# mLSTM heads of a hybrid layer: token sums by a two-column stationary operand, factors turned by DRAM, and carried keys weighted and summed on VectorE

## The chip, the core and the metric

The kernel runs on one core of one Trainium2 chip. The metric is device time in microseconds (us) of one execution, the median of several runs; lower is better. Engines are named as in the profile: PE (TensorE matmuls), PEld (its weight loads), DVE (VectorE), ACT (ScalarE), POOL (GpSimd), SP (SyncE, which issues every DMA here).

## The reference, cut to what matters

The layer runs four mLSTM heads and eight forgetting-attention heads side by side on 1024 tokens of width 1024, then a projection, cross-attention into 256 memory tokens, a squared-ReLU MLP and a final norm. The change is in the mLSTM heads (128 wide each), which the reference computes so:

```python
def body(carry, xs):
    C, n, m = carry
    ...
    scores = jnp.einsum('bhtd,bhsd->bhts', qc, kc) * jnp.exp(dmat - m_t[..., None])
    inter = jnp.exp(m_inter - m_t)
    num = (jnp.einsum('bhts,bhsd->bhtd', scores, vc)
           + inter[..., None] * jnp.einsum('bhed,bhtd->bhte', C, qc))
    den = scores.sum(-1) + inter * jnp.einsum('bhd,bhtd->bht', n, qc)
    h = num / jnp.maximum(jnp.abs(den), jnp.exp(-m_t))[..., None]
    ...
    C_new = decay[..., None, None] * C + jnp.einsum('bhs,bhse,bhsd->bhed', wa, vc, kc)
    n_new = decay[..., None] * n + jnp.einsum('bhs,bhsd->bhd', wa, kc)
...
mh = mh * lax.rsqrt(jnp.mean(mh * mh, axis=-1, keepdims=True) + EPS)
mh = mh * ml_norm[l].astype(jnp.float32).reshape(ML_HEADS, ML_DH)
ml_out = (mh.reshape(B, S, ML_W) * jax.nn.sigmoid(ml_o.astype(jnp.float32))).astype(x.dtype)
```

For each token two sums are needed: `den`, a sum over the weighted scores, and the mean square of the head's 128 outputs. Together they give one factor per token and head.

## The kernel before

Activations lie with the model's width on the partitions and tokens along the free axis. A matmul of fp32 accuracy is three passes over operands that are split into a high and a low part (`mm3`, lines 184 to 188); the split itself is an ACT copy that rounds (L134 or L137) and a DVE subtraction (L135 or L138). A projection tile of 128 outputs by 512 tokens is 24 matmuls of 512 columns into one PSUM bank. Banks are handed out by `mm()` in the rotation mm, tp, m2, tp: a bank is free again when DVE has taken the last result out of it.

An mLSTM head is worked in two halves of 512 tokens, each a chunk of its own. For each head `ml_project` runs the key projection, its convolution and SiLU (`conv_silu`, L505 to L513), a forgetting-attention projection, `carried` (the state after the first half), the query projection with its convolution, another forgetting-attention projection, `carry` (state times queries of the second half: L557, L562, L563) and the output gate. Then `ml_head` (a generator) does the scores and sums of both halves; its closing part, which scales the outputs by the factors and stores them, is stepped between the pieces of the next head's `ml_project` (`closing`, `next(closing)`), and for the last head between pieces of the attention's value projection.

Inside `ml_head`, per half: scores into PSUM (`sp`), weights by ACT (L587, from the row broadcast `nmb` in tile r_a, loaded by L576), a mask by POOL (L589), the product by DVE (L590), the split, the running sum `acc` by POOL (L594) and the weighted values into `num` (bank ov). After the last key block come `nsb` (L600), its square `sq` (L601), and `sum_cols` (L217) on `acc` and on `sq`: for each 128 tokens a matmul with those 128 columns as stationary operand and the constant column `ones` moving, so that a sum lands as one column with 128 tokens on the partitions. Eight columns of `dens` and of `sqs` hold the 1024 tokens of a head. The factor `fac` comes out of these (L612 to L618) as 128 by 8; `to_row` (L249 to L253) turns it with a PE transpose, an ACT copy, a store to DRAM (`facd`) and a broadcast load into r_a, and L626 loads the second half's broadcast. L629, L630, L137 and L138 make the scaled output and its split, L633 and L634 store it to `mix`.

`carried` (L519 to L552) transposes the keys y on PE (L527), multiplies them by weights per token on DVE while it takes them out of PSUM (L529), splits them, multiplies them with the values (L540), and sums them per key dimension with four more matmuls against `ones` (L542).

Tile buffers are few: r_a and r_y have one each, r_c, r_d, r_e and r_p two each, the PSUM score bank `sc` three. The framework orders each engine's instructions ahead of time; what stands in a row waits for what stands above it on that engine, DMA issues on SP too. SP keeps a strict order: an issue whose data are not ready holds those behind it.

## Time and profile before

| | us |
|---|---|
| median of 3 runs | 1521.66 (1521.24 to 1523.61) |
| the profiled execution: its time | 1523.35 |
| the profiled execution: its span in the trace | 1521.6 |
| DVE busy | 1100.3 (72%) |
| ACT busy | 727.7 (48%) |
| POOL busy | 510.1 (34%) |

The span runs from the first to the last instruction of the trace; what lies around it is 1.75 us of this execution's time. The mLSTM heads fill roughly 80 to 390 us of the span; the score phase of the forgetting attention runs beside the last head's end from about 355 us on. The lines that carry the argument stand in the prediction.

### The profile page before, as it was taken

What the parts mean: (1) busy time and instruction counts of PE and PEld (TensorE: products, weight loads), DVE (VectorE), ACT (ScalarE), POOL (GpSimd) and SP (SyncE); (2) the same over time, 40 slices, a digit from 0 to 9 for tenths busy, and PEclk for the clock granted to TensorE, in tenths of its full rate; (3) what the DMA queues carried; (4) which work ended last, traced back from release to release, by engine and by line L of the source; (5) the groups of instructions that cost most, each with busy time, mean ns of one, the idle gap of its engine ahead of it and who ended that gap; (6) DMA issues with size and microseconds to landing.
All of it is one profiled execution on the core that took longest, in us unless ns stands there. A gap on an engine that the chain in (4) does not pass through costs nothing.

```text
span 1521.6 us, 21977 instructions
## 1 busy us (share of the span) xinstructions
PE 1502.7 (99%) x7694; PEld 1261.5 (83%) x7694; DVE 1100.3 (72%) x1743; ACT 727.7 (48%) x1360; POOL 510.1 (34%) x543
## 2 busy tenths in 40 slices
PE   9999999999999999999999999999999999999997
PEld 9988888889999788888888877778787888888887
DVE  7766676765787786944457989898887667787665
ACT  7324343334687665644443456666664621122124
POOL 1003030413364442511110034544555265663322
PEclk9999999999999999999999999999999999999999
DMA  6322223435888886843344437776678777776623
GB/s 239 109 77 87 98 100 114 135 126 157 246 244 267 260 264 230 300 131 124 119 147 157 153 134 277 247 256 242 222 252 286 291 277 276 276 270 248 239 94 111
DMA packets 122538, 299.86 MB, mean 197 GB/s; under 512 B 13614, under 2 KB 28264, under 8 KB 115516
## 3 DMA queue, kind: packets, MB, share of 16 engines
q1 hardware_dynamic: 122428, 298.46, 57.4%
q8 instruction: 60, 0.98, 0.3%
q14 instruction: 50, 0.41, 0.1%
HBM read 199.60 MB, written 98.81 MB: 196 GB/s over the span
## 4 chain that ended last, share of the span: by engine, by line
PE 93%; DVE 3%; ACT 2%; DMA 1%; issue 1%; SPq 0%; DVEq 0%; POOLq 0%; POOL 0%; ACTq 0%
PE tp L186 8%; PE tp L187 8%; PE tp L188 8%; PE m L186 6%; PE sc L186 6%; PE m L187 6%; PE m L188 6%; PE sc L187 6%; PE sc L188 6%; PE mm L186 6%; PE mm L187 6%; PE mm L188 6%; PE ov L186 2%; PE ov L187 2%; PE ov L188 2%; PE ov L801 2%
## 5 line engine op out<-in xcount | busy, mean ns | idle before, releaser
L186 PE MATMUL tp<-act,wl 128*128 128x512 f32 (+1 forms) x440 | 172.9, 393 | 1.2 <-ACT row L1396 0.7
L187 PE MATMUL tp<-act,wh 128*128 128x512 f32 (+1 forms) x440 | 172.1, 391 | 0.0
L188 PE MATMUL tp<-act,wh 128*128 128x512 f32 (+1 forms) x440 | 171.7, 391 | 0.0
L135 DVE TENSOR_TENSOR wl<-wr,wh 128x1024 fp32r<-128x1024 f32 (+2 forms) x95 | 124.5, 1311 | 22.0 <-ACT wh L134 21.4
L134 ACT ACTIVATE wh<-wr 128x1024 fp32r<-128x1024 f32 (+2 forms) x95 | 95.6, 1007 | 75.9 <-PE tp L188 34.7
L186 PE MATMUL mm<-act,wl 128*128 128x512 f32 (+1 forms) x332 | 127.5, 384 | 0.0
L188 PE MATMUL mm<-act,wh 128*128 128x512 f32 (+1 forms) x332 | 127.3, 383 | 0.0
L187 PE MATMUL mm<-act,wh 128*128 128x512 f32 (+1 forms) x332 | 127.2, 383 | 0.0
L186 PE MATMUL m<-act,wl 128*128 128x512 f32 (+1 forms) x308 | 117.7, 382 | 0.5 <-DVE wl L135 0.5
L188 PE MATMUL m<-act,wh 128*128 128x512 f32 (+1 forms) x308 | 117.7, 382 | 0.0
L187 PE MATMUL m<-act,wh 128*128 128x512 f32 (+1 forms) x308 | 117.5, 381 | 0.0
L186 PEld LDWEIGHTS tp<-act,wl 128*128 128x128 f32 x440 | 82.6, 188 | 20.6 <-ACT row L1396 1.2
L188 PEld LDWEIGHTS tp<-act,wh 128*128 128x128 f32 x440 | 82.6, 188 | 18.9
L187 PEld LDWEIGHTS tp<-act,wh 128*128 128x128 f32 x440 | 82.7, 188 | 18.5
L186 PE MATMUL sc<-act,wl 128*128 128x512 f32 (+1 forms) x248 | 97.0, 391 | 1.0 <-DVE wl L135 1.0
L188 PE MATMUL sc<-act,wh 128*128 128x512 f32 (+1 forms) x248 | 96.7, 390 | 0.0
L187 PE MATMUL sc<-act,wh 128*128 128x512 f32 (+1 forms) x248 | 96.6, 390 | 0.0
L1467 POOL TENSOR_TENSOR z<-wr 128x256 f32<-128x256 f32 x56 | 51.7, 944 | 130.6 <-DMA wr<-w_ff2q 116.8
L134 ACT ACTIVATE wh<-z 128x1024 fp32r<-128x1024 f32 (+1 forms) x54 | 55.5, 1028 | 80.8 <-POOL z L1467 58.4
L135 DVE TENSOR_TENSOR wl<-z,wh 128x1024 fp32r<-128x1024 f32 (+1 forms) x54 | 74.3, 1376 | 7.8 <-ACT wh L134 7.6
L134 ACT ACTIVATE w<-wr 128x768 fp32r<-128x768 f32 (+2 forms) x31 | 25.5, 823 | 106.2 <-PE tp L186 33.7
L188 PEld LDWEIGHTS mm<-act,wh 128*128 128x128 f32 x332 | 62.3, 188 | 12.7
(726 smaller groups left out, 4288.4 us busy)
## 6 DMA issues: line engine op xcount, KB each, us to landing
act<-right SPq DMA_DIRECT2D x49, 1024.0 KB
right<-w SPq DMA_DIRECT2D x56, 256.0 KB
wr<-w_ff2q SPq DMA_DIRECT2D x28, 512.0 KB
right<-r_d SPq DMA_DIRECT2D x49, 256.0 KB
right<-r_e SPq DMA_DIRECT2D x49, 256.0 KB
act<-fqk SPq DMA_DIRECT2D x48, 256.0 KB
wr<-w_in SPq DMA_DIRECT2D x20, 512.0 KB
wr<-w_ff SPq DMA_DIRECT2D x20, 512.0 KB
```

The costliest lines, as they stand in the source:

```text
L134: s.activation(hi, src, AF.Copy)
L135: return v.tensor_tensor(out=lo, in0=src, in1=hi.bitcast(F32), op=ALU.subtract)
L186: nc.tensor.matmul(ps, w[1], x[0], start=first, stop=False, skip_group_check=more)
L187: nc.tensor.matmul(ps, w[0], x[1], start=False, stop=False, skip_group_check=more)
L188: nc.tensor.matmul(ps, w[0], x[0], start=False, stop=last, skip_group_check=more)
L801: nc.tensor.matmul(self.ov[:, c0:], self.fv[:, self.j], t[:, c0:], start=self.j == 0 and t is self.p[1], stop=self.last and t is self.p[0])
L1467: g.tensor_tensor(out=o, in0=x, in1=y, op=op)
```

## The change

Four things change.

1. The sums over partitions: `acc` and `sq` are now split into a high and a low part as any other operand, and four matmuls per half, each with a two-column constant `pick` as stationary operand and 512 tokens moving, put both sums as two rows of 512 into one bank. `pick` has the columns (1, 0) for the first pair and (0, 1) for the second. ACT copies the two rows to r_y, and SP stores them to a DRAM tensor `sumd`.
2. The factors: both sums of all 1024 tokens of a head are loaded back from `sumd` with eight tokens a partition, the factor is computed in that layout after the generator's first `yield` (before: ahead of it), stored straight to `facd`, and both halves are loaded as broadcasts. The PE transpose, its ACT copy and `to_row` are gone. `emc`, exp of minus the running maximum, goes by DRAM into the same layout once (`tops`), in place of eight small PE transposes.
3. `carried`: the weights of the first 512 keys are loaded as a broadcast from DRAM (`rels`) into r_c, ACT takes their exponential (512 wide), and one DVE instruction multiplies the keys by them and sums along the tokens, which gives `n_`. The weighted keys are then transposed, and the split is taken straight from PSUM. The four `ones` matmuls and the DVE multiplication from PSUM are gone.
4. Every factor of a head goes through DRAM in both directions now (`sumd`, then `facd`).

```diff
 def carried(hd, y):
-        s.activation(wc, gcol[:, 0:4, hd], AF.Exp, bias=m0)
-        v.tensor_scalar(out=wc, in0=wc, scalar1=0.5 * float(P) ** -0.5, scalar2=None, op0=ALU.mult)
+        yw = w2("c")
+        load(yw, rels[hd : hd + 1].broadcast_to([P, TH]))
+        s.activation(yw, yw, AF.Exp, bias=m0)
+        v.tensor_tensor_reduce(out=yw, in0=y[:, :TH], in1=yw, scale=0.5 * float(P) ** -0.5, scalar=0.0, op0=ALU.mult, op1=ALU.add, accum_out=n_)
...
-            nc.tensor.transpose(kt[:, j * P : (j + 1) * P], y[:, j * P : (j + 1) * P], ident)
-        kw = w2("c")
-        v.tensor_tensor(
...
+            nc.tensor.transpose(kt[:, j * P : (j + 1) * P], yw[:, j * P : (j + 1) * P], ident)
         kh, kl = w2("d", dt=F32R), w2("e", dt=F32R)
-        split(kh, kl, kw)
+        split(kh, kl, kt)
...
-        for j in range(4):
-            nc.tensor.matmul(ps[:, 256:257], kw[:, j * P : (j + 1) * P], ones, start=j == 0, stop=j == 3, skip_group_check=True)
...
 def ml_head(hd, q, k, og, num1, den1):
+            sh, sl = w2("d", dt=F32R), w2("e", dt=F32R)
+            split(sh, sl, acc)
...
-            ps = sc()
-            sum_cols(ps[:, 0:4], acc, 4)
-            sum_cols(ps[:, 4:8], sq, 4)
-            s.activation(dens[:, 4 * hf : 4 * hf + 4], ps[:, 0:4], AF.Abs)
-            v.tensor_copy(sqs[:, 4 * hf : 4 * hf + 4], ps[:, 4:8])
+            sq, qh, ql = w2("c"), w2("d", dt=F32R), w2("e", dt=F32R)
+            s.activation(sq, src, AF.Square)
+            split(qh, ql, sq)
+            ps = sc()[:2]
+            for e, parts in enumerate(((sl, sh), (ql, qh))):
+                for x in parts:
+                    nc.tensor.matmul(ps, pick[:, 2 * e : 2 * e + 2], x, start=x is sl, stop=x is qh)
+            two = w2("y", p=2)
+            s.activation(two, ps, AF.Copy)
+            load(sumd[hd, :, hf * TH : hf * TH + TH], two)
             nums.append(nsb)
+        both_ = col("dens", 16).rearrange("p (e i) -> p e i", e=2)
+        load(both_, along(sumd[hd]))
+        dens, sqs = both_[:, 0], both_[:, 1]
+        yield
+        s.activation(dens, dens, AF.Abs)
...
-        yield
+        at = facd[hd : hd + 1]
+        load(along(at)[:, 0], fac)
         for hf in range(2):
             fb = w2("a")
-            at = facd[hd : hd + 1]
-            if hf == 0:
-                to_row(fb, fac, 8, at, sc)
-            else:
-                load(fb, at[:, TH:].broadcast_to([P, TH]))
+            load(fb, at[:, hf * TH : hf * TH + TH].broadcast_to([P, TH]))
             yield
```

`along` is `x.rearrange("h (p i) -> p h i", i=8)`; `load` is SP's DMA start for loads and stores alike. The lines after the change are numbered anew: 603 for 600 (`nsb`), 610 for 601 (`sq`), 512 to 520 for 505 to 513, 639 and 640 for 629 and 630, 643 for 633.

The order of the instructions moves with it. On PE, at the end of head 1's sums (between the projections of head 2; mm, m and tp are projection banks, ov the weighted values, r_d and r_e splits, act_106 and act_107 the values), there stood before:

```order
L188 MATMUL mm_2215<-act_102,wh_2209 128x512
L217 MATMUL sc_1981<-ones,r_c_1978 128x1 x4
L186 MATMUL m_330_2282<-act_102,wl_2279 128x512
L187 MATMUL m_330_2282<-act_103,wh_2278 128x512
L188 MATMUL m_330_2282<-act_102,wh_2278 128x512
```

Five more matmuls of that tile m follow before the state's first matmul (L540). Now:

```order
L187 MATMUL ov_1917<-r_e_1975,act_106 128x256
L188 MATMUL ov_1917<-r_d_1974,act_106 128x256
L615 MATMUL sc_1993<-r_e_1983,pick 2x512
L615 MATMUL sc_1993<-r_d_1982,pick 2x512
L615 MATMUL sc_1993<-r_e_1989,pick 2x512
L615 MATMUL sc_1993<-r_d_1988,pick 2x512
L536 MATMUL m_328_2179<-ident,r_c_2175 128x128 x4
L542 MATMUL tp_2188<-act_107,r_e_2185 128x256
L542 MATMUL tp_2188<-act_107,r_d_2184 128x256
```

The projection's matmuls that stood between the last `ov` work, the sums (L217, now L615) and the state's matmuls (L540, now L542) are gone from between them: the transposes (L536) and the state follow the sums at once. At the same place of the heads 0 and 2 a whole projection tile still stands ahead of L615 and another between L536 and L542.

On DVE, a little later in the same head (c_fac is the factor, r_a its broadcast, z the projected queries of head 2, tp_2241 and tp_2246 the bank of their second half), before:

```order
L208 SCALAR_TENSOR_TENSOR c_fac_1827<-c_t_2001,c_y_1999 128x8
L545 TENSOR_TENSOR r_c_2192<-tp_2179,r_c_2192 128x128
L549 TENSOR_SCALAR c_m_2164<-tp_2179 128x1
L618 TENSOR_TENSOR c_fac_1827<-c_fac_1827,c_rd_1993 128x8
L135 TENSOR_TENSOR r_p_2195<-r_c_2192,r_p_2195 128x128
L505 TENSOR_TENSOR z_323_2213<-tp_2241,row 128x512
L508 TENSOR_SCALAR z_326_2267<-z_323_2213,vec 128x1024
L135 TENSOR_TENSOR wl_2601<-wr_2598,wh_2600 128x1024
L510 SCALAR_TENSOR_TENSOR z_326_2267<-z_323_2213,vec,z_326_2267 128x1024
L629 SCALAR_TENSOR_TENSOR r_f_1897<-r_f_1897,vec,r_a_2079 128x512
```

and now:

```order
L206 TENSOR_TENSOR c_t_2086<-c_y_2084 128x8
L135 TENSOR_TENSOR r_p_2200<-r_c_2197,r_p_2200 128x128
L207 SCALAR_TENSOR_TENSOR c_t_2086<-c_t_2086,c_var_2082 128x8
L208 SCALAR_TENSOR_TENSOR c_fac_1828<-c_t_2086,c_y_2084 128x8
L631 TENSOR_TENSOR c_fac_1828<-c_fac_1828,c_rd_2078 128x8
L639 SCALAR_TENSOR_TENSOR r_f_1899<-r_f_1899,vec,r_a_2092 128x512
L640 SCALAR_TENSOR_TENSOR r_f_1899<-w_240_1767,r_f_1899 128x512
L512 TENSOR_TENSOR z_338_2218<-tp_2246,row 128x512
L515 TENSOR_SCALAR z_341_2272<-z_338_2218,vec 128x1024
```

The scaling of head 1 by the loaded factor (L629, L630; now L639, L640) stood behind the taking out of the projection's second half (L505) and the convolution's start; now it stands ahead of that (L512).

On SP, at the end of the last head (fvd is the attention's value store, r_a the factors' broadcast, r_y and r_f the scaled output), before:

```order
L251 DMA facd<-r_a_3228 8x128
L653 DMA fvd<-r_c_3626 128x4x128
L849 DMA w_589_3839<-fvd 128x1024
L253 DMA r_a_3228<-facd 128x512
L653 DMA fvd<-r_b_3655 128x4x128
L626 DMA r_a_3323<-facd 128x512
L653 DMA fvd<-r_p_3684 128x4x128
L1094 DMA act_3833<-hmd 128x4096
L633 DMA mix<-r_y_3318 128x512
```

and now:

```order
L633 DMA facd<-c_fac_3015 128x8
L663 DMA fvd<-r_c_3730 128x4x128
L726 DMA act_3195<-fqk 64x1024 x3
L985 DMA wr_3921<-w_xv 128x1024
L663 DMA fvd<-r_b_3759 128x4x128
L726 DMA act_3195<-fqk 64x1024
L636 DMA r_a_3249<-facd 128x512
L663 DMA fvd<-r_p_3788 128x4x128
L663 DMA fvd<-r_c_3817 128x4x128
L663 DMA fvd<-r_b_3846 128x4x128
L636 DMA r_a_3340<-facd 128x512
L643 DMA mix<-r_y_3335 128x512
```

Between the store of the factor and the load of its broadcast three stores of value tiles, four loads of attention operands and a weight load now stand; the second broadcast stands behind three more value tiles.

## The prediction

> **What bounds the kernel now.** The page first: who is busy, and what the chain that ended last is made of.

> ```profile
> span 1521.6 us, 21977 instructions
> PE 1502.7 (99%) x7694; PEld 1261.5 (83%) x7694; DVE 1100.3 (72%) x1743; ACT 727.7 (48%) x1360; POOL 510.1 (34%) x543
> PEclk9999999999999999999999999999999999999999
> PE 93%; DVE 3%; ACT 2%; DMA 1%; issue 1%; SPq 0%; DVEq 0%; POOLq 0%; POOL 0%; ACTq 0%
> ```

> PE is the bound and runs at its full granted clock. Next the stretches where the change lies (columns: stretch, length, then busy of PE, PEld, DVE, ACT, POOL, clock, DMA), and PE's waits, once for the whole run and once for 80 to 400 us (total, times, longest).

> ```profile
> 80.00:340.00 260.00, 260.00 (x1276) 216.79 (x1274) 172.92 (x261) 95.41 (x155) 50.17 (x62) 1.00 0.32 107
> 340.00:400.00 60.00, 59.43 (x473) 57.60 (x471) 33.89 (x95) 28.85 (x76) 22.50 (x30) 1.00 0.68 192
> 400.00:440.00 40.00, 38.55 (x286) 35.97 (x285) 32.19 (x83) 31.87 (x85) 21.31 (x31) 1.00 0.84 240
> ...
> PE ov L129 <- POOL ident L118: 1.9, 1, 1.9
> ```

> ```profile
> PE tp L782 <- DVE r_b L138: 0.5, 1, 0.5
> ```

> In 260 us of mLSTM work PE never waits. So what is removed from PE is gained one to one, and every wait that comes up there is lost one to one: the forecast is PE work removed against PE pauses added. No pause is longer than 1.9 us.

> **PE's own work.** The sums of one group (four program matmuls, eight passes in fp32) between 512-column matmuls:

> ```profile
> 231.76 0.95 PE L217 MATMUL sc<-ones,r_c 128*128 128x1 f32 x8
> 232.56 0.48 PE L186 MATMUL m<-act,wl 128*128 128x512 f32 x1
> 232.88 0.39 PE L187 MATMUL m<-act,wh 128*128 128x512 f32 x1
> 233.11 0.40 PE L188 MATMUL m<-act,wh 128*128 128x512 f32 x1
> ...
> L217 PE MATMUL sc<-ones,r_b 128*128 128x1 f32 x64 | 8.4, 218 | 0.0
> L217 PE MATMUL sc<-ones,r_c 128*128 128x1 f32 x64 | 7.6, 239 | 0.0
> L249 PE MATMUL sc<-ident,c_fac 128*8 128x128 f32 x4 | 1.1, 274 | 0.0
> ```

> A 512-column matmul takes 233.11 - 232.88 = 0.23 us from start to start. From 231.76 to 232.88 are 1.12 us, of which one such is L186's, so a group costs 0.89. The 128 passes are 16 groups: 14.2 us. The state's `ones` matmuls (L542) have the same form, four groups, 3.6. Eight small transposes in `gate_cols` and four of `fac` are about 1.0 together (an estimate from L249: start to start, at most its mean). Removed: 18.8. Added: 4 matmuls of 512 columns per half, 32 in all, at 0.233: 7.5. That a two-column stationary operand makes the pass no cheaper is assumed: the pass streams the same 512 columns. Net **-11.3 us**. This is certain within 1 us; the rest is about pauses.

> **The squeeze after head 1's sums.** There the order now has `ov`, sums, transposes, state on end, on PE. What was three tasks beside each other becomes one chain: `nsb` (L603), its square (ACT), the split (ACT, DVE), the keys' product with sum (L532, queued behind these on DVE), transposes, their split, state. The rows of before:

> ```profile
> 226.53 0.49 PE L527 MATMUL m<-ident,z 128*128 128x128 f32 x3
> ```

> ```profile
> 227.35 0.69 DVE L600 TENSOR_TENSOR r_f<-ov,r_f 128x512 f32<-128x512 f32 x1
> 229.94 0.69 DVE L135 TENSOR_TENSOR r_e<-r_c,r_d 128x512 fp32r<-128x512 f32 x1 [0.70 <-ACT r_d L134]
> ...
> 399.04 0.68 DVE L744 CUSTOM_DVE_ANT_0 sc<-sc,causal 128x512 f32<-128x512 f32 x1
> 399.63 0.14 DVE L744 DVE_READ_ACCUMULATOR2_ANT c_mx<- 128x1 f32 x1
> ```

> ```profile
> 228.15 0.63 ACT L601 ACTIVATE r_c<-r_f 128x512 f32<-128x512 f32 x1 [1.46 <-DVE r_f L600]
> 229.27 0.64 ACT L134 ACTIVATE r_d<-r_c 128x512 fp32r<-128x512 f32 x1 [0.48 <-DVE r_c L529]
> ```

> Chain: 0.69 + 0.63 + 0.64 + 0.69 for the square's split; L532 is not in the trace, its nearest row is L744, the same kind with an accumulated result, 0.68 + 0.14 = 0.82; four transposes about 0.5 (three show 0.49 to their modelled end); split 0.64 + 0.69; in sum 5.3, and eight hand-offs of 0.03 to 0.11 (228.15 after 228.04; 229.94 after 229.91), 0.5. PE's own work in these 5.8 us is 4 x 0.23 + 0.43 = 1.4. Pause 4.4; DVE still has an earlier split and a projection row ahead of L603, up to 1 us. I take **+5.0** (4.4 to 5.4). The bank of the next projection tile stands behind the state's, so nothing fills it. In the heads 0 and 2 two tiles of 24 x 0.233 = 5.6 us lie between, more than each half of the chain: no pause from this.

> **The factors' way through DRAM.** Two round trips, and DVE and ACT wait for both in order. Rows (SP issues, then DVE):

> ```profile
> 68.54 0.34 SPq L521 DMA_DIRECT2D c_m<-rows  x1
> ...
> 173.16 0.29 SPq L251 DMA_DIRECT2D facd<-r_a  x1
> 176.20 0.33 SPq L253 DMA_DIRECT2D r_a<-facd  x1
> ...
> 242.31 0.29 SPq L251 DMA_DIRECT2D facd<-r_a  x1
> 243.53 0.33 SPq L253 DMA_DIRECT2D r_a<-facd  x1
> ...
> 256.58 0.32 SPq L521 DMA_DIRECT2D c_m<-rows  x1
> ```

> ```profile
> 71.05 0.15 DVE L550 TENSOR_SCALAR c_m<-c_m 128x1 f32<-128x1 f32 x1 [1.54 <-DMA c_m<-rows]
> ...
> 232.95 0.16 DVE L610 COPY c_sqs<-sc 128x4 f32<-128x4 f32 x1 [0.30 <-ACT c_dens L609]
> 237.07 0.15 DVE L618 TENSOR_TENSOR c_fac<-c_fac,c_rd 128x8 f32<-128x8 f32 x1
> 242.25 0.69 DVE L505 TENSOR_TENSOR z<-tp,row 128x512 f32<-128x512 f32 x1 [4.49 <-PE tp L188]
> 246.80 0.75 DVE L629 SCALAR_TENSOR_TENSOR r_f<-r_f,vec,r_a 128x512 f32<-128x512 f32 x1 [0.68 <-DMA r_a<-facd]
> 256.74 1.23 DVE L138 SCALAR_TENSOR_TENSOR w<-z,w 128x1024 fp32r<-128x1024 f32 x1 [0.19 <-ACT w L137]
> 260.21 0.15 DVE L550 TENSOR_SCALAR c_m<-c_m 128x1 f32<-128x1 f32 x1 [1.64 <-DMA c_m<-rows]
> ```

> ```profile
> 260.01 0.39 PE L186 MATMUL mm<-w,r_p 128*128 128x512 f32 x1
> ```

> A small store until the load behind it may issue: 1.2 to 3.0, I take 2.1. A load of small pieces until its user starts: `c_m`, 2.5 and 3.6, I take 3.0. The broadcast: 246.80 - 243.53 = 3.3, I take 3.1. From sums to factor: 237.22 - 232.95 = 4.3.

> Head 1, from the end of the last `ov` (t = 0): sums complete at 4.5 (first half of the chain above with its hand-offs and backlog, 3.9, then two matmuls), copy 5.2, `sumd` there and back 10.3, factor 14.7, `facd` there and back 19.9, L639 and L640 21.3. Only then does DVE take the projection's second half (L512), whose bank PE has filled at 5.0 + 0.9 + 0.4 + 0.9 + 5.6 = 12.8. It is 8.5 late, 7.1 net of L639 and L640, which stood later in that path before. Before, the path from L505 to the queries' high part (ACT L137, released just before L138 at 256.74) ended 3.3 ahead of the state's matmul at 260.01. So PE pauses **+3.8** at `carry` (1.5 with hops of 1.2 and 2.5, 6.4 with 3.0, 3.6 and 3.3).

> Heads 0 and 2 have the same two trips with the fillers beside them: there L639 stands behind the convolution, and only the low split and what follows can be late. r_a has one buffer, so the next head's row broadcast (L578) and its first exponentials start only after the second L639. **+1.0** for head 0 (0 to 2), **+3.0** for head 2, where the value projection's banks wait for the same DVE queue (0.5 to 4.5).

> **The last head's end.** The factors now meet the attention's score phase. Between the factor's store and the broadcast's issue SP has eight other issues, and DVE's L639 stands behind the last value tiles. The scaled halves share the one r_y, so the second waits for the first one's store:

> ```profile
> 383.04 0.32 SPq L633 DMA_DIRECT2D mix<-r_y  x1
> ```

> ```profile
> 393.97 0.63 ACT L137 ACTIVATE r_y<-r_f 128x512 fp32r<-128x512 f32 x1 [3.65 <-DMA mix<-r_y]
> ```

> That store took 393.97 - 383.04 = 10.9 us, ACT stood 3.65 for it, and it cost PE nothing, as value projections lay there. Now it falls among score tiles, whose exponentials are on the same ACT queue. The second L137 is due some 4.4 after the first store's issue (L639, L640 and the score rows between them), so ACT stands 10.9 - 4.4 = 6.5; three score banks give PE about 1.5: 5.0. With 2.0 for `c_dens` and factor waits in the order of 340 to 400 us: **+7.0** (2, if the store takes 5 us, to 10).

> **Sum.** -11.3 + 5.0 + 3.8 + 1.0 + 3.0 + 7.0 = +8.5: span 1530.1. The profiled execution lies 1.7 over its span and over the median, so the median moves from 1521.66 to **1530**.

> ACT's and DVE's added rows, per half two splits (0.64 and 0.69 each) and per head a 512-wide exponential, have room (DVE 172.92 of 260); they count only where named. The new loads (256 KB per head) add little to a DMA share of 0.32.

> **Rivals.** (1) *Everything hides.* For it: PE waits nowhere today. Against: the orders above leave no filler. 1521.7 - 11.3 = 1510.4; chance 0.04. (2) *Only the squeeze costs*, the DRAM trips stay beside PE's banked work: -11.3 + 5.0, 1515.4, faster. For it: L629 waits for `facd` today (246.80) without harm. Against: two trips instead of one, and L512 behind them. It decides if a round trip takes under some 3.2 us, 1.9 less than I take; the shortest rows add to 3.7. Chance 0.06. (3) *Short hops*: all at their low ends, the last store at some 9 us: -11.3 + 4.4 + 1.5 + 0 + 0.5 + 5 = 0.1, no change, 1522; chance 0.12. (4) *Long hops*: all high: -11.3 + 5.4 + 6.4 + 2 + 4.5 + 10 = +17, 1538.7; chance 0.15. (5) *The clock falls in the new pauses.* The granted clock is 1.00 in all stretches, but no pause was over 1.9. If it halves for as long as each of three pauses (5, 4, 5) lasted, PE loses 7 more: 1537; chance 0.08. [...] The forecast keeps 0.55.

> [...]

> **Range and chances.** A measurement tells about 0.2% (3.0 us) from no change: faster is under 1518.6, slower over 1524.7. Rivals 1 and 2 are faster (0.10). Rival 3 is mostly the same, and the forecast's low edge adds a little: 0.13. Slower: 0.77. Low end 1520.5 takes in rival 3, high end 1537.5 most of 4 and 5.

> **What would show it.** PE busy about 1491; PE waits at L542 and L615 near 233 to 237 us (about 5 in all), at the state's matmul of head 2's `carry` (about 4) and at score matmuls near 415 to 425, released by ACT; ACT's L137 on r_y waiting for `mix`; DVE L639 waiting for `facd`, ACT L624 for `sumd`. If PE's 80 to 340 us shows no wait over 1 us, the chains are wrong and the time is near 1510 to 1515. If the sums' new matmuls take more than 0.23 each, the first term is wrong.

## The result, and the profile after

| | before | after |
|---|---|---|
| median of 8 runs each, us | 1521.68 | 1526.29 (1524.92 to 1533.20) |
| ratio, 95% interval | | 1.0037 (1.0023 to 1.0052) |
| the profiled execution: its time, its span | 1523.35, 1521.6 | 1525.55, 1523.8 |

The change makes the kernel slower by 4.6 us, on the forecast's side and inside its range; the forecast was 1530. The profiled execution is one of the shorter of the eight. The page of after, with the lines that answer to those shown of before:

```profile
span 1523.8 us, 21780 instructions
PE 1495.2 (98%) x7554; PEld 1245.4 (82%) x7554; DVE 1113.9 (73%) x1751; ACT 740.7 (49%) x1376; POOL 512.5 (34%) x546
```

The same three stretches as before (length, busy time of PE, PEld, DVE, ACT, POOL, granted clock, DMA share, GB/s), and PE's waits:

```profile
80.00:340.00 260.00, 253.60 (x1175) 205.21 (x1174) 177.56 (x263) 104.10 (x165) 53.90 (x61) 1.00 0.34 107
340.00:400.00 60.00, 55.69 (x428) 52.32 (x426) 33.54 (x86) 30.99 (x78) 21.29 (x27) 1.00 0.73 205
400.00:440.00 40.00, 37.92 (x265) 34.87 (x266) 35.24 (x91) 30.68 (x80) 21.36 (x30) 0.96 0.74 214
```

```profile
PE sc L615 <- DVE r_e L135: 2.9, 2, 2.1
PE tp L792 <- DVE r_e L135: 2.7, 1, 2.7
...
PE tp L542 <- DVE r_e L135: 1.4, 1, 1.4
...
PE tp L186 <- DVE r_f L562: 1.0, 1, 1.0
PE ov L186 <- ACT r_d L134: 1.0, 1, 1.0
```

PE, which before had waited 0.5 us at most in 80 to 400 us, now waits 1 us or more at four places (the three waits of the squeeze counted as one; L792's ends at 400.4), and at 400 to 440 us the clock is no longer full. Busy time runs to modelled ends, so a wait in this list is some 0.16 us shorter than what PE loses from start to start (0.39 busy against 0.233 for 512 columns). For the accounts below the loss was therefore counted from starts: for each PE instruction the time to the next start, less the usual spacing of its kind (0.233 us for 512 columns, 0.118 for 256). That gives 1493.1 us of work and 20.1 of loss before, 1481.7 and 33.2 after:

| term | forecast | measured |
|---|---|---|
| PE's own work | -11.3 | -11.4 |
| head 0 (120 to 160 us) | +1.0 | +1.0 |
| squeeze after head 1's sums (200 to 240) | +5.0 | +5.1 |
| `carry` of head 2 (240 to 280) | +3.8 | 0 |
| head 2 (280 to 360) | +3.0 | +3.5 |
| last head's end (360 to 440) | +7.0 | +5.8 |
| all other stretches | 0 | -2.3 |
| sum | +8.5 | +1.7 |

The +1.7 is that of the profiled execution from the first matmul to the last (its whole span grew by 2.2); the rest of the median's 4.6 is in the runs, which spread over 8.3 us after the change and 2.5 before. Both are taken up below.

The squeeze, on PE's timeline of after (start, duration; in brackets the idle time and what ended it):

```profile
226.48 0.28 PE L188 MATMUL ov<-r_d,act 128*128 128x256 f32 x1
228.88 0.40 PE L615 MATMUL sc<-r_e,pick 128*2 128x512 f32 x1 [2.12 <-DVE r_e L135]
229.11 0.40 PE L615 MATMUL sc<-r_d,pick 128*2 128x512 f32 x1
230.33 0.39 PE L615 MATMUL sc<-r_e,pick 128*2 128x512 f32 x1 [0.82 <-DVE r_e L135]
...
230.97 0.66 PE L536 MATMUL m<-ident,r_c 128*128 128x128 f32 x4
233.04 0.39 PE L542 MATMUL tp<-act,r_e 128*128 128x256 f32 x1 [1.41 <-DVE r_e L135]
```

From 226.48 to 233.04 are 6.56 us; the work in it is 0.12 + 4 x 0.233 + some 0.43 for the transposes, 1.5: 5.1 lost. The two-column operand costs the 0.23 us assumed (229.11 - 228.88). The last head's end, on the timelines of PE, of DVE and of SP's issues:

```profile
400.40 0.33 PE L792 MATMUL tp<-ident,w 128*128 128x128 f32 x1 [2.71 <-DVE r_e L135]
```

```profile
399.13 0.75 DVE L639 SCALAR_TENSOR_TENSOR r_f<-r_f,vec,r_a 128x512 f32<-128x512 f32 x1 [2.80 <-DMA r_a<-facd]
399.80 0.55 DVE L135 TENSOR_TENSOR r_e<-tp,r_d 128x384 fp32r<-128x384 f32 x1
```

```profile
381.12 0.33 SPq L1104 DMA_DIRECT2D act<-hmd  x1
...
381.98 0.50 SPq L633 DMA_DIRECT2D facd<-c_fac  x1
...
391.10 0.58 SPq L636 DMA_DIRECT2D r_a<-facd  x1
```

PE waits for a split on DVE, and that split stands in DVE's queue behind L639, which waits for the factor. The factor's store was issued 0.86 us behind a 2 MB load (L1104); its broadcast could be issued 9.1 us later and reached DVE 8.0 us after that. In head 1 the same two steps take 1.4 and 3.0 (below). The DMA packets in the trace show where these times went: the load's 128 packets of 16 KB started from 382.08 to 388.66 us, the store's 128 packets of 32 bytes only from 388.93 to 390.08, and the broadcast's 128 packets of 2 KB from 395.94 to 398.53, behind 4 KB packets of the loads issued ahead of it (L726, L985). So the store stood behind the 2 MB, and the broadcast behind what had piled up meanwhile. Right after this pause the clock falls to half (windows of after, cut where it changes):

```profile
398.85:402.26 3.41, 1.30 (x7) 0.90 (x8) 3.13 (x10) 0.91 (x2) 0.93 (x2) 1.00 0.52 157
402.26:405.67 3.41, 3.36 (x16) 3.07 (x16) 3.41 (x9) 2.35 (x6) 1.74 (x5) 0.50 0.57 164
405.67:409.09 3.42, 3.40 (x28) 3.08 (x27) 3.00 (x7) 2.57 (x6) 2.11 (x2) 1.00 0.99 326
```

For 3.41 us PE ran at half: 1.7 us of its work lost without any wait in the list. Why just there is taken up under e11.

### The profile page after: what moved, and what is told of

Read it like the earlier page. It is cut to its first block, busy times and chain, and to the rows that moved or that the text cites. A ratio compares the mean times of both kernels' runs of the same rounds, so it can differ in the third digit from the quotient of the medians.

```text
span 1523.8 us, 21780 instructions
## 1 busy us (share of the span) xinstructions
PE 1495.2 (98%) x7554; PEld 1245.4 (82%) x7554; DVE 1113.9 (73%) x1751; ACT 740.7 (49%) x1376; POOL 512.5 (34%) x546
## 5 line engine op out<-in xcount | busy, mean ns | idle before, releaser
L186 PE MATMUL tp<-act,wl 128*128 128x512 f32 (+1 forms) x440 | 172.4, 392 | 1.2 <-ACT row L1406 0.7
L187 PE MATMUL tp<-act,wh 128*128 128x512 f32 (+1 forms) x440 | 171.8, 390 | 0.0
L188 PE MATMUL tp<-act,wh 128*128 128x512 f32 (+1 forms) x440 | 171.4, 391 | 0.0
L135 DVE TENSOR_TENSOR wl<-wr,wh 128x1024 fp32r<-128x1024 f32 (+2 forms) x95 | 123.7, 1302 | 23.0 <-ACT wh L134 22.3
L134 ACT ACTIVATE wh<-wr 128x1024 fp32r<-128x1024 f32 (+2 forms) x95 | 95.6, 1006 | 89.6 <-PE tp L188 39.5
L186 PE MATMUL mm<-act,wl 128*128 128x512 f32 (+1 forms) x332 | 127.7, 385 | 0.5 <-DVE r_p L652 0.3
L188 PE MATMUL mm<-act,wh 128*128 128x512 f32 (+1 forms) x332 | 127.6, 384 | 0.0
L187 PE MATMUL mm<-act,wh 128*128 128x512 f32 (+1 forms) x332 | 127.3, 384 | 0.0
L186 PE MATMUL m<-act,wl 128*128 128x512 f32 (+1 forms) x308 | 117.9, 383 | 0.8 <-DVE r_p L652 0.3
L188 PE MATMUL m<-act,wh 128*128 128x512 f32 (+1 forms) x308 | 117.5, 381 | 0.0
L187 PE MATMUL m<-act,wh 128*128 128x512 f32 (+1 forms) x308 | 117.4, 381 | 0.0
L186 PEld LDWEIGHTS tp<-act,wl 128*128 128x128 f32 x440 | 82.6, 188 | 20.7 <-ACT row L1406 1.2
L188 PEld LDWEIGHTS tp<-act,wh 128*128 128x128 f32 x440 | 82.6, 188 | 19.1
L186 PE MATMUL sc<-act,wl 128*128 128x512 f32 (+1 forms) x248 | 96.9, 391 | 1.1 <-DVE wl L135 0.8
L187 PEld LDWEIGHTS tp<-act,wh 128*128 128x128 f32 x440 | 82.6, 188 | 18.6
L188 PE MATMUL sc<-act,wh 128*128 128x512 f32 (+1 forms) x248 | 96.5, 389 | 0.0
L187 PE MATMUL sc<-act,wh 128*128 128x512 f32 (+1 forms) x248 | 96.4, 389 | 0.0
L134 ACT ACTIVATE wh<-z 128x1024 fp32r<-128x1024 f32 (+1 forms) x54 | 55.5, 1027 | 83.2 <-POOL z L1477 60.5
L135 DVE TENSOR_TENSOR wl<-z,wh 128x1024 fp32r<-128x1024 f32 (+1 forms) x54 | 74.9, 1387 | 7.7 <-ACT wh L134 7.4
L134 ACT ACTIVATE w<-wr 128x768 fp32r<-128x768 f32 (+2 forms) x31 | 25.5, 823 | 104.0 <-PE tp L186 32.6
L186 PEld LDWEIGHTS mm<-act,wl 128*128 128x128 f32 x332 | 62.8, 189 | 13.0 <-DVE r_p L652 0.6
```

The lines of the kernel that those rows point to most:

```text
L134: s.activation(hi, src, AF.Copy)
L135: return v.tensor_tensor(out=lo, in0=src, in1=hi.bitcast(F32), op=ALU.subtract)
L186: nc.tensor.matmul(ps, w[1], x[0], start=first, stop=False, skip_group_check=more)
L187: nc.tensor.matmul(ps, w[0], x[1], start=False, stop=False, skip_group_check=more)
L188: nc.tensor.matmul(ps, w[0], x[0], start=False, stop=last, skip_group_check=more)
```

## The experiments

All ratios are to before on the same chip, with the 95% interval. The kernels ran on several chips, and before's median beside them was 1522.97 (e1 to e4), 1522.18 (e5 to e10) and 1523.04 us (e11, e12), against 1521.68 beside the change. So a difference in us between two kernels of different sets is good to some 1.5 us only; the ratios are the better measure.

**One half of the change alone.** Kernel e1 is the change with the old `carried` (DVE multiplies the transposed keys by `wc`, four `ones` matmuls); e2 is before with the new `carried` and the old sums.

> The change with the state of the first half (carried) as it was before: raw keys transposed, weighted on VectorE out of PSUM, four ones matmuls. Theory (PE work removed against pauses at three named places): the keys' chain no longer stands behind the splits of head 1's sums, so the 4.35 us of pauses at 228.9 to 233.0 us shrink to under 1; PE saves 11.3 - 3.6 = 7.7 us; the pauses of the last head's end (about 4 us and 1.7 us of half clock) stay. 1521.7 - 7.7 + 7 = 1521, range 1518 to 1524. Rival (the new sums themselves are slow, by ACT's and VectorE's added splits, and the keys' part is harmless): the pauses at 229 to 233 us stay and the time is 1526 + 3.6, about 1530.

> The kernel before with the new carried alone (weights by a broadcast load, product and sum in one VectorE instruction, transposes of weighted keys); sums and factors as before. Theory: PE saves the four ones groups, 3.6 us; the chain at head 1's end is shorter than in the change (no splits of the sums ahead of it on VectorE), a pause of 1 to 2.6 us stays there; nothing changes at the last head's end. 1521.7 - 3.6 + 2 = 1520, range 1518.5 to 1521.5. Rival (the keys' chain alone makes the squeeze): pauses of 4 us or more there and 1522 or over.

Measured: e1 1523.77, ratio 1.0006 (0.9997 to 1.0015); e2 1528.43, ratio 1.0039 (1.0026 to 1.0051). In e1 PE's work is 7.9 us less than before, and 80 to 320 us have no pause: the squeeze is gone with the new keys, as the theory had it, and the time lies at the upper end of its range. What e1 gains is spent at the last head, by a wait and by a clock of 0.83 in 400 to 420 us (PE's waits of e1, 4.8 of it at 403.6 us):

```profile
PE sc L751 <- ACT act L773: 6.7, 5, 4.8
```

Followed back, that wait ends at the factor's way too: ACT's exponential stands behind a copy that waits for DVE, and DVE there stands behind the second scaling (399.46), which waits for the second broadcast, issued at 394.37.

For e2 the theory was wrong and its rival right: the keys alone make a squeeze, by another link (ACT's timeline of e2, then PE's):

```profile
231.78 0.72 ACT L526 ACTIVATE r_c<-r_c,c_m 128x512 f32<-128x512 f32 x1 [3.73 <-DMA r_c<-rels]
```

```profile
233.28 0.66 PE L531 MATMUL m<-ident,r_c 128*128 128x128 f32 x4 [1.78 <-DVE c_m L527]
235.35 0.58 PE L537 MATMUL tp<-act,r_e 128*128 128x256 f32 x1 [1.41 <-DVE r_e L135]
```

ACT waits 3.7 us for the broadcast of the weights, and the chain exponential, product with sum, transposes, split, state runs on end behind it. Two pauses of 1.8 and 1.4, and behind them 6.83 us at half clock (234.03 to 240.85 by its windows), in which PE was busy for 5.5 us, so that some 2.7 us of its work were lost: nearly as much as the pauses. Two more pauses, of 1.1 and 1.7, stand at 301.7 and 310.1 us, the second by the same link in the next head.

**What keeps PE from filling the squeeze.** e3 is the change with the key transposes in a score bank, so that they take no projection bank from the rotation:

```diff
-        kt = mm() if hd else sc()
-        turn[0] += hd == 0
+        kt = sc()
+        turn[0] += 1
```

> The change, with the transposed weighted keys of every head in a bank of the scores instead of a bank of the projections' rotation. Theory: the next projection tile has a bank while the chain sums, transposes, split runs, so of the 4.35 us of pauses at 229 to 233 us about 1.8 stay; the rest of the change unmoved: 1526.3 - 2.5 = 1524, down to 1521 if the order of the last head's end moves too. Rival (the splits on ACT and VectorE set the pace there, not the bank): pauses of 4 us again and 1526 within 1.

Measured: 1521.20, ratio 0.9992 (0.9982 to 1.0001), 5.1 under the change. Of the squeeze one wait is left (PE's timeline of e3; the sums stand between projection matmuls again):

```profile
236.18 0.39 PE L542 MATMUL tp<-act,r_e 128*128 128x256 f32 x1 [1.44 <-DVE r_e L135]
```

So the bank rotation decided the squeeze: the chain has the same steps, but PE has a tile to work on. At the last head e3 waits 5.8 us (L792 for DVE) at 394.5. Its SP order there is of use below: the factor's store and first broadcast are issued at 374.25 and 376.68, ahead of the 2 MB load (377.11), and take 2.4 and 5.0 us; the second broadcast is issued at 382.43, behind the load, and DVE's second scaling starts at 392.60, 10.2 us later.

**The last head without DRAM trips.** e4 is the change with the old sums and factor (`sum_cols`, `to_row`) for the last head alone (the eight small PE transposes of `emc` come back with them):

```diff
+            if hd == MLH - 1:
...
+                sum_cols(ps[:, 0:4], acc, 4)
+                sum_cols(ps[:, 4:8], sq, 4)
...
+            if last_head and hf == 0:
+                to_row(fb, fac, 8, at, sc)
```

> The change for heads 0 to 2; the last head's sums by ones matmuls and its factor by a PE transpose as before, without the trip of the sums through DRAM. PE has 1.7 us more for the sums and 0.5 for small transposes. Theory (the last head's pauses come from VectorE's L639, which waits for the factor's way through DRAM behind the 2 MB load): the pause of 2.7 us near 400 us and the 3.4 us of half clock behind it (worth 1.7) go, 1526.3 + 2.2 - 5 = 1523.5, range 1521 to 1525. Rival (the last head's loss is noise of the attention's own order, or clock alone): the pause near 400 stays or another takes its place, 1527 to 1529.

Measured: 1524.13 (1519.97 to 1528.82), ratio 1.0008 (0.9997 to 1.0019). The pause at 400 us and the clock's fall there are gone from the profile, at 2.3 us more PE work. The squeeze's waits stay (2.1, 0.8 and 1.4). Its eleven runs spread over 8.9 us, and the mean granted clock over the whole run tells the shortest apart: 1519.97 and 1520.38 have 0.998, the other nine, from 1523.48 on, 0.996 or less. A mean lower by 0.002 is 6 us at half clock, 3 us of time. (One of the nine shows 0.944 at 1524.30 us; that would be some 80 us more of lost work than its neighbours have, which its time doesn't show, so that one record is most likely wrong.)

**The squeeze filled.** e5 is e4 with 15 matmuls without use at the squeeze, nine ahead of head 1's second sums and six ahead of the state, 3.5 us of PE work:

```diff
+            if hd == 1 and hf:
+                for _ in range(9):
+                    nc.tensor.matmul(ps, pick[:, 0:2], h[0][0][:, 0], start=True, stop=True)
...
+        if hd == 2:
+            for _ in range(6):
+                nc.tensor.matmul(ps, h[0][0][:, 0, 0:P], h[0][0][:, 0], start=True, stop=True)
```

> The last-head-as-before kernel (e4), plus 15 matmuls whose results nothing uses (9 of two columns by 512 into the sums' bank of head 1, 6 of 128 by 512 into the state's bank of head 2, 3.5 us of PE). They move the order: a projection tile stands between the transposes and the state at head 1's end again. Theory (the pauses there cost twice: their own length, and in most executions a half clock for 3.4 to 6.8 us behind them): without pauses over 1 us before 340 us the executions lie close together, near e4's fastest two, median 1520 (1518.5 to 1521.5) against e4's 1524, although PE does 3.5 us more. Rival (the spread of the executions comes from elsewhere, the pauses cost their length alone): 1524.1 - 4.3 + 3.5, 1523 or over, with the same spread as e4.

Measured: 1520.90 (1519.74 to 1522.48), ratio 0.9988 (0.9979 to 0.9996): 3.2 under e4 (3.0 by the ratios, as the chips differ) with more work on PE. The order moved with the fillers (projection tiles stand in the squeeze too), so the squeeze's pauses are gone by both; what the run shows is the spread: mean clock 0.997 or 0.998 in all eleven runs, and 2.7 us between the ends instead of 8.9. That is what the theory asked for; that the clock alone makes e4's spread is not shown by it.

**Old keys again, in all heads or in head 2 alone**, with the old sums in the last head (e6, e7):

```diff
-        state = carried(hd, yk)
+        state = (carried_old if hd == 2 else carried)(hd, yk)
```

> New sums and factors in heads 0 to 2, the keys' part as before in all heads, and the last head's sums and factor as before. PE saves 7.9 - 2.3 = 5.6 us by count. Theory: no pause over 1 us in 80 to 330 us, none at the last head's end beyond those of before, so the gain stays: 1521.7 - 5.6 + 1 = 1517, range 1515 to 1519. Rival (ACT's and VectorE's added splits and the DRAM trips cost in some other place): 1520 or over.

> As e6, but with the new keys' part in heads 0, 1 and 3, where a projection tile lies between its steps, and the old one only in head 2, where the change left none. PE saves 8.2 us by count. Theory: some 2 us of pause stay at the sums of head 1, 1 to 2 at head 2's end: 1521.7 - 8.2 + 3 = 1516.5, range 1514.5 to 1519.5; with a half clock behind the pause in some executions. Rival (the keys' broadcast load into r_c is late in every head): pauses at the transposes of the heads 1 and 3, 1520 or over.

Measured: e6 1521.07, ratio 0.9991 (0.9979 to 1.0002); e7 1520.80, ratio 0.9987 (0.9979 to 0.9996). Both missed on the high side by some 4 us. In e6 a score matmul waits 1.8 for ACT at 387.5 and the clock of 380 to 400 us is 0.91; e7 has 1.7 at head 1's sums and 1.9 among the scores, between 480 and 520 us. Each edit moves the whole order, and small pauses come up at places where no edit was made; why just there stays open.

**Both cures.** e8 is e3 and e4 together.

> The change with the transposed keys in a score bank (as e3) and the last head's sums and factor as before (as e4). PE saves 9.1 us by count. Theory: e3's pause of 5.8 us near 394 us goes with the factor's way, pauses of 0.7, 0.8 and 1.4 us stay at 178, 198 and 236 us: 1521.7 - 9.1 + 3.5 = 1516, range 1514 to 1519. Rival (e3's late pause came from the bank's change): another pause of over 3 us after 380 us, 1520.

Measured: 1519.31 (1517.90 to 1522.37), ratio 0.9981 (0.9972 to 0.9989), just over the range expected. Pauses left: 0.7 at 198.5 and 1.4 at 236.7.

**A longer hop.** e9 is the change with one more copy through DRAM for the sums of the heads 0 to 2:

```diff
-        load(both_, along(sumd[hd]))
+        if hd < MLH - 1:
+            load(sumd2[hd], sumd[hd])
+            load(both_, along(sumd2[hd]))
```

> The change with one more trip in heads 0 to 2: the sums are copied from sumd to a second DRAM tensor before they are loaded back, so that the factor comes some 2 us later. Theory (the trips are covered in the change only because they are short: at head 2's carry the queries' high part was ready 0.9 us before PE needed it): PE pauses 1 to 2 us at that matmul near 258 us, by ACT or VectorE, and VectorE's L644 shows that much more wait for facd; time 1527 to 1530 against 1526.3. Rival (the trips have several us to spare): no pause there, 1526 within 1.

Measured: 1533.25, ratio 1.0075 (1.0061 to 1.0088), 7 over the change (5.8 by the ratios): the size is there, the place is not. The copy puts the load behind it off by 2.0 us (234.03 to 236.02 on SP), DVE's first scaling starts 3.4 us later than in the change (242.90 there), and `carry` of head 2 has no pause still: DVE's L644 starts at 246.33, PE's matmul at 261.98 without a wait. PE had been held up itself: pauses that add up to 5.2 between 226 and 235 us and a clock of 0.83 in 220 to 240 brought it to this matmul 3.6 us later than in the change (258.36). So the trial could not settle what a late factor costs at `carry`. Most of the rest is at the last head, where the trip was not changed: a pause of 5.2 at 410.6 and a clock of 0.74 in 400 to 420.

**The best.** e10 is e8 with the old keys in head 2.

> e8 (transposed keys in a score bank, last head's sums and factor as before) with the old keys' part in head 2, the one place where e8 still pauses 1.4 us. PE saves 8.2 us by count. Theory: no pause over 1 us in 80 to 380 us and no half clock there: 1521.7 - 8.2 + 1.5 = 1515, range 1513.5 to 1517.5, executions close together. Rival (new sums and splits cost VectorE and ACT so much that another place pauses): 1518 or over.

Measured: 1516.77 (1516.56 to 1518.28), ratio 0.9969 (0.9957 to 0.9981): faster than before and than the change, and as expected. The clock is full from 200 to 430 us, and at the last head PE has no pause beyond two of 0.4 us (at 391 and 396), where before has 0.5 and 0.4:

```profile
400.00:420.00 20.00, 20.00 (x146) 18.52 (x145) 16.27 (x45) 15.94 (x47) 10.94 (x15) 1.00 0.57 171
```

**The load ahead of the factor.** e11 is the change with the 2 MB load issued behind the last head's first factor broadcast; e12 puts that, instead of the old sums, into e10.

```diff
-    load(hm.bitcast(F32), hmd)
+    with tc.issue_after(spreads[-1].ins):
+        load(hm.bitcast(F32), hmd)
```

> The change, with one difference: the 2 MB load of the normalized memory (L1104), which stood on SP just ahead of the last head's factor store, is issued behind that head's first factor broadcast. Theory (the pause at 400 us is DVE's L639 waiting for a factor that went through a full DMA queue: in the change every transfer issued from 381 to 393 us took 7 to 9 us, the factor's store 8.8 and its broadcast 8.0): with the 2 MB behind it the store takes 1.5 to 3 us and the broadcast 3 to 5, L639 starts at least 6 us earlier than 399.13, the pause of 2.71 us ahead of L792 and the half clock from 402 to 405.6 us go, and the median falls by 2.7 + 0.6 + 1.7 = 5 from the change's 1526.3 to about 1521.5 (1520 to 1524). Rival A (the other loads keep the queue full): the two hops stay over 12 us together, the pause stays, 1526. Rival B (the wait moves: the 2 MB arrive late for the first key product near 404 us, or the score loads behind them do): L639 is early, but a pause of 2 us or more stands at a score matmul or at the first mm matmul after 396 us, 1524 or over.

> The best kernel so far (two-column sums, keys carried by VectorE in all heads but head 2, key transposes in the sc banks, 1516.77 us) with the changed kernel's way for the last head too, and the 2 MB load behind its first factor broadcast, instead of the old sums in that head. Theory: with the load out of the way the last head's DRAM trips are hidden, so its PE work, 2.3 us less (nominal 1481.7 in the change against 1484.0 with the old sums in the last head), is gained: 1514.5 to 1516.5. Rival (the trips cost there whatever the load does, through the order on DVE and ACT): a pause of 1.5 us or more between 380 and 410 us, and 1517.5 or over.

Measured: e11 1530.67 (1528.58 to 1532.99), ratio 1.0053 (1.0036 to 1.0070); e12 1521.22, ratio 0.9988 (0.9979 to 0.9998). Both forecasts missed. Of e11's rivals, B had the wait move and its time, but named other transfers than the one that came late; e12's rival had the pause and the time. e11 shows what holds L639 (SP's issues, DVE's two scalings and PE in e11):

```profile
383.31 0.33 SPq L634 DMA_DIRECT2D facd<-c_fac  x1
...
385.93 0.33 SPq L637 DMA_DIRECT2D r_a<-facd  x1
386.36 0.38 SPq L1108 DMA_DIRECT2D act<-hmd  x1
...
391.63 0.33 SPq L637 DMA_DIRECT2D r_a<-facd  x1
```

```profile
390.86 0.75 DVE L642 SCALAR_TENSOR_TENSOR r_f<-r_f,vec,r_a 128x512 f32<-128x512 f32 x1 [3.96 <-DMA r_a<-facd]
...
402.77 0.75 DVE L642 SCALAR_TENSOR_TENSOR r_f<-r_f,vec,r_a 128x512 f32<-128x512 f32 x1 [6.42 <-DMA r_a<-facd]
```

```profile
404.18 0.69 PE L795 MATMUL tp<-ident,w 128*128 128x128 f32 x2 [6.45 <-DVE r_e L135]
```

Ahead of the load, store and broadcast take 2.6 and 4.9 us, and the first scaling starts 8.3 us earlier than in the change. But the second half's broadcast needs the one buffer r_a, so it is issued only after that, now behind the 2 MB, and takes 11.1 us. The pause moved from the first scaling to the second and grew from 2.7 to 6.5. In e11 and e3 alike the transfers issued ahead of the load take 2.4 to 5.0 us and the one behind it 11.1 and 10.2. The wait is the factor's queueing behind the load and what is issued with it, wherever it falls. e12 pauses 5.8 us at 394.5, as e3 does, and for the same reason: the order that e12's edit asks for, the load behind the first broadcast, is the one that e3 already had, so e3's trace had shown what would come of it. A version in which both broadcasts stand ahead of the load (a second r_a) was not tried.

**The clock, from all profiles together.** e11 shows something more by chance. Its squeeze has the change's waits to 0.01 us, but not its clock (PE's timeline of e11; then windows of e11, and of after at the same place):

```profile
228.58 0.40 PE L616 MATMUL sc<-r_e,pick 128*2 128x512 f32 x1 [2.12 <-DVE r_e L135]
230.03 0.40 PE L616 MATMUL sc<-r_e,pick 128*2 128x512 f32 x1 [0.82 <-DVE r_e L135]
233.23 0.58 PE L542 MATMUL tp<-act,r_e 128*128 128x256 f32 x1 [1.41 <-DVE r_e L135]
```

```profile
227.55:230.96 3.41, 1.41 (x5) 0.33 (x6) 2.52 (x6) 2.25 (x4) 0.00 (x0) 1.00 0.16 37
230.96:234.37 3.41, 2.00 (x9) 1.60 (x9) 0.69 (x1) 0.95 (x3) 0.00 (x0) 0.50 0.09 20
234.37:237.79 3.42, 3.42 (x12) 2.84 (x11) 1.60 (x9) 1.38 (x4) 1.65 (x1) 0.50 0.20 65
```

```profile
224.77:228.18 3.41, 1.99 (x12) 1.55 (x10) 3.41 (x7) 1.03 (x2) 0.00 (x0) 1.00 0.68 207
228.18:231.59 3.41, 1.87 (x8) 0.59 (x8) 2.13 (x6) 2.48 (x4) 0.00 (x0) 1.00 0.10 34
231.59:235.01 3.42, 2.01 (x13) 1.81 (x13) 0.90 (x3) 0.97 (x3) 0.00 (x0) 1.00 0.17 43
```

The stretches at half clock in the eight profiles that have any between 200 and 430 us are 3.41, 6.83 or 10.24 us long, one, two or three times 3.41; and where one execution has two of them, their starts are a multiple apart (e9: 231.00 and 408.48, 177.48 = 52 x 3.413; e11: 230.96 and 401.62, 170.66 = 50 x 3.413). In the change's profile the fall at 402.26 and the half clock at the end of the run (from 1515.00) are 326 x 3.413 apart. So each of these executions can be divided into periods of 3.41 us, counted from one of its falls (the windows above are such periods), and each period's idle time on PE set beside the clock of the next one. In the eight profiles, from 70 to 560 us, 43 periods at full clock have over 0.7 us idle: after all 32 with up to 1.66 idle the clock stays, and after 10 of the 11 with 1.76 or more it halves (the one of 1.88, in e3, is followed by a full idle period and then by the fall). These eight were picked because their clock falls. The other six profiles, divided in the same way, have 19 more such periods, and one of them, in e4, has 1.77 us idle and is followed by full clock (its window):

```profile
225.70:229.11 3.41, 1.64 (x10) 1.26 (x9) 3.41 (x7) 0.95 (x3) 0.00 (x0) 1.00 0.50 175
```

So in all fourteen none of 50 periods with up to 1.66 us idle is followed by a fall, two of the four from 1.76 to 1.88 are, and all eight from 2.00 on; more than that these profiles don't show. In e11 two waits of the squeeze fall into one such period (3.41 - 1.41 = 2.00 idle), and half clock follows; in the change's profiled execution the most idle period there has 1.54, and the clock stays at 1.00. The instructions and the waits are the same there, but e11 starts the first of these sums 0.30 us earlier than the change and the matmul of `carry` 2.22 us later (260.58 against 258.36): 2.5 us more, with the same waits and another clock.

## Why the prediction was right, and where it was not

**PE's own work: right** (-11.4 for -11.3).

**The squeeze: right** in place, chain and size. The bank of the next tile was named as what leaves PE without work, and e3 shows it.

**Heads 0 and 2: right in size** (1.0, and 3.5 for 3.0), and in part in mechanism. The waits of head 2 are two of 1.0, for DVE's L562 at 337 us and for ACT's split at 347, and two of 0.3 and 0.2 at 293.5 and 300.3, as head 0 has them. The first one comes by the link that the prediction named, the row broadcast that waits for the one buffer r_a: the second L639 starts at 328.79, the broadcast (L578) is issued at 329.57, and ACT's first exponential waits for it:

```profile
334.23 0.72 ACT L589 ACTIVATE r_b<-r_a,gcol 128x512 f32<-128x512 f32 x1 [6.21 <-DMA r_a<-rows]
```

Behind that stand ACT's L137 (334.86), DVE's L138 (335.50) and L562 (336.24), and PE at 336.99. The second comes by a link that it did not name: ACT's split stands behind an L137 (346.05) that had waited 2.3 us for a store of r_p to `fqk`. No run takes either of them away.

**`carry` of head 2: wrong, 0 for +3.8.** The step that failed is the length of the DRAM trips. SP's issues, and the first users on ACT and DVE, in after:

```profile
231.60 0.25 SPq L618 DMA_DIRECT2D sumd<-r_y  x1
232.82 0.37 SPq L621 DMA_DIRECT2D c_dens<-sumd  x1
...
238.45 0.32 SPq L633 DMA_DIRECT2D facd<-c_fac  x1
239.86 4.14 SPq L636 DMA_DIRECT2D r_a<-facd  x2
```

```profile
234.53 0.21 ACT L624 ACTIVATE c_dens<-c_dens 128x8 f32<-128x8 f32 x1 [2.27 <-DMA c_dens<-sumd]
```

```profile
242.90 0.75 DVE L639 SCALAR_TENSOR_TENSOR r_f<-r_f,vec,r_a 128x512 f32<-128x512 f32 x1 [4.47 <-DMA r_a<-facd]
```

The stores take 1.2 and 1.4, the small load 1.7, the broadcast 3.0: 7.4 for both trips, where the prediction took 10.3. The small load was priced by `c_m`, 2.5 and 3.6 us for 4 bytes a partition; with two pieces of 32 bytes a partition it took about half of that, and why was not tested. L512 then starts at 244.29, 17.5 us after the last `ov` (226.48 + 0.28), where 21.3 was forecast: 3.8 sooner, 2.9 by the trips and 0.9 by the sums and the factor, and 3.8 was the whole pause. The queries' high part is ready at 256.38 + 1.07 = 257.45, PE's matmul starts at 258.36: the slack fell from 3.3 to 0.9 us and holds. The rival of short hops stands closer to this term than the forecast did.

```profile
256.38 1.07 ACT L137 ACTIVATE w<-z 128x1024 fp32r<-128x1024 f32 x1 [0.34 <-DVE z L520]
```

```profile
258.36 0.40 PE L186 MATMUL mm<-w,r_p 128*128 128x512 f32 x1
```

**The last head's end: right place, wrong mechanism, and the size (5.8 for 7.0) near by luck.** ACT's second L137 was to stand 6.5 us for the store of r_y, which had taken 10.9 before, and PE 5 of them; ACT waits for no `mix` now:

```profile
406.47 0.63 ACT L137 ACTIVATE r_y<-r_f 128x512 fp32r<-128x512 f32 x1 [1.33 <-issue]
```

What waits is DVE's L639, for a factor behind the 2 MB load. The prediction counted the eight issues between store and broadcast, but gave the factor's wait 2 us and the store of r_y 5. The step that failed is that it took the 10.9 us for the store's own length. In before, SP had issued the same 2 MB load 0.84 us ahead of that store (383.04), and both factor broadcasts ahead of the load (375.90 and 380.79):

```profile
382.20 0.50 SPq L1094 DMA_DIRECT2D act<-hmd  x1
```

In the change the load is issued just ahead of the factor's store, so the delay fell on the factor, and the store of r_y (401.77) came after it. e4 takes the pause away, and e11 moves it with the load. The predicted link does exist: in e1 ACT's second L137 waits 0.7 us for the first store (397.16 to 405.61), and PE 1.3 us behind it, at 407.0.

**The clock: the rival's mechanism is there, in part.** The prediction kept the clock at full and gave its fall 0.08, with 7 us for three places. In the profiled execution it fell at one and cost 1.7; at the squeeze it stayed at 1.00 in this execution and fell for 6.83 us in e11's. That makes 2.5 us between two executions with the same waits, and is most likely a part of the median's 4.6 over the profile's 1.7. It isn't all: the mean clock of the change's eight runs goes with their times only loosely (0.998 at 1525.46, 0.994 at 1528.36, 0.995 at 1533.20), and no other execution of it was profiled. The 7 us took the clock to halve for as long as each pause lasts, which no run shows: the stretches at half clock measured were 3.41, 6.83 or 10.24 us long, and PE had been idle for 1.76 us of the 3.41 ahead of one in e6 (one wait) and for 2.00, made up of two waits, in e11.

**Not foreseen:** the other stretches give back 2.3 us, most of it behind 440 us, where the score phase has waits of its own (one of 1.3 us between 460 and 520 in before, where the change has 0.5). Most likely they overlap with the delay, so that a delay ahead of a part that waits anyway isn't lost in full; this was not tested. The forecast added all terms one to one to the end.

In sum, of the 6.8 us between the forecast's sum and the profiled execution's, 3.8 are the `carry` term, 2.3 what is absorbed elsewhere, and 1.2 the last head's end, less 0.5 at head 2. The median came nearer to the forecast (4.6 of 8.5) than the profiled execution did (1.7), by a spread between runs that the forecast had no term for.

## What to carry to other kernels

Where one engine is full, work taken off it is gained only if the order still has something for it to do while the longer chain runs: count the chain, then look for the tile and its bank that can fill the gap. Pauses of 1 to 2 us can cost twice, by the wait and by the clock behind it (in e11, 2.00 us idle within 3.41 were followed by 6.83 us at half clock), and may show as a spread between runs before they show in one profile (8.9 us between the ends in e4, 2.7 in e5). A 4 KB store on a chain is better not queued behind a 2 MB load (9.1 us until its reader's issue, against 1.4 in head 1), and a long transfer in a trace should first be read for what was issued ahead of it; and when the load is moved, the second small transfer that shares a single buffer with the first must be moved past as well.
